# Issuing the last store of a relu-and-sum kernel from ScalarE instead of SyncE

## The chip, the cores and the metric

The kernel runs on one core of a Trainium2 chip. A core has several engines with instruction streams of their own: here VectorE (DVE) and ScalarE (ACT) compute, and SyncE (SP) issues the transfers (DMAs) between the main memory (HBM) and the on-chip memory (SBUF, 128 partitions). The engines are tied together by semaphores: an instruction raises one when it is done, another waits until it has reached a value; a DMA raises its semaphore by 16 when all of it has landed. The metric is the device time of one execution in microseconds (us); less is better.

## The reference

```python
def setup_inputs():
    batch, seq, dim = 32, 512, 1024
    return {"x": np.random.randn(batch, seq, dim).astype(np.float32)}

def reference(x):
    relu_x = np.maximum(x, 0)
    return np.sum(relu_x, axis=-1).astype(np.float32)
```

There are 32 x 512 = 16384 rows of 1024 floats. Each row is clipped at zero and summed to one number. 67 MB go in, 64 KB come out.

## The kernel before

A row is worked on inside one partition, so each of the 128 partitions has J = 128 rows and J results, which are collected in `res` (128 x 128). The rows are divided into three regions of 1, 111 and 16 rows per partition (`REGIONS`), and each region has a store of its own at the end.

The input comes in seven big chunks of 16 rows per partition (8 MB each), into three buffers in turn, and then in a tail of 8, 4 and 2 rows (`TAIL`). The last two rows are cut into four pieces, so that little work is left when the last byte arrives: 912 columns, 512 columns, 256 columns, and a piece of 368 columns that crosses from the one row into the other and goes into a buffer called `seam`. All loads are issued by SP (lines 85 to 115); from the fourth chunk on, SP first waits until DVE has read the buffer that the load is to overwrite.

In the first six chunks ACT clips in place (line 145) and DVE sums (line 160). From the seventh on both engines work on rows of their own: one instruction clips a row and adds it up, followed by a short instruction that reads the accumulator (ACT by `on_act`, line 127; DVE by `on_dve`, line 130).

The end is written out by hand in lines 187 to 209. ACT and DVE each sum half of the 912 columns into `seam` (semaphore `s_half`), ACT the 512 columns and DVE the 256 columns also into `seam` (`s_seam`). Then each engine has one closing instruction, which sums a part of `seam` with those partial sums in it: ACT's gives the result of row J - 2, DVE's that of row J - 1 (lines 201 and 203). Each of the two raises `s_last` by 1.

There are three stores, all issued by SP before the change: the first region in a transposed form (line 117, after `s_turn`), the second region's 111 columns of `res` (line 123, after both engines are done with the last big chunk and the last input piece has landed), and the last region's 16 columns, 8 KB in all (line 207, once `s_last` has reached 2). The first two raise `s_store`, the last one `s_out`. SP ends by waiting for both.

Of the kernel before, what the change touches and what calls it, by code (L numbers as in the profile page):

```python
# [16 lines left out]
def bass_relu_sum_kernel(  # L17
# [20 lines left out]
    J = B * S // P  # L38
# [5 lines left out]
    start = [sum(REGIONS[:i]) for i in range(len(REGIONS))]  # L44
# [4 lines left out]
    ov = [of[P * s : P * (s + n)].rearrange("(p j) -> p j", p=P) for s, n in zip(start, REGIONS)]  # L49
# [4 lines left out]
    res = nc.alloc_sbuf_tensor("res", [P, J], fp32)  # L54
# [10 lines left out]
    s_last = nc.alloc_semaphore("s_last")  # L65
    s_turn = nc.alloc_semaphore("s_turn")
    s_store = nc.alloc_semaphore("s_store")
    s_out = nc.alloc_semaphore("s_out")

    sp, act, dve = nc.sync, nc.scalar, nc.vector  # L70
# [14 lines left out]
    for c in range(NBIG + 1):  # L85
        if c >= NB:
            sp.wait_ge(s_dve, done[c - NB])
        if c < NBIG:
            i = 0
            for g, j, n in CHUNKS[c]:  # L90
                sp.dma_start(  # L91
                    out=buf[:, c % NB, i : i + n, :], in_=xv[g][:, j : j + n, :]
# [18 lines left out]
    for k, (lo, hi) in enumerate((first, second, third)):  # L111
# [6 lines left out]
        out=of[0:P].rearrange("(k q) -> k q", q=32), in_=turned[0:P:32, 0:32]  # L118
# [7 lines left out]
    def on_act(t, acc):  # L126
        return act.activation(t, t, AF.Relu, accum_out=acc)  # L127

    def on_dve(t, acc):
        return dve.tensor_scalar(  # L130
            out=t, in0=t, scalar1=0.0, scalar2=None, op0=ALU.max, op1=ALU.add, accum_out=acc
        )
# [5 lines left out]
    for c in range(NTWO):  # L138
# [17 lines left out]
        for n in DVE_STEPS[c]:  # L156
            if ready[r + n - 1] > seen:
# [3 lines left out]
                out=res[:, c * BIG + r : c * BIG + r + n],  # L161
                in_=buf[:, c % NB, r : r + n, :],
# [36 lines left out]
    act.wait_ge(s_seam, 16 + 2)  # L199
    act.wait_ge(s_half, 2)  # L200
    on_act(seam[:, 0:k], res[:, J - 2 : J - 1]).then_inc(s_last, 1)
    dve.wait_ge(s_seam, 16 + 2)
    on_dve(seam[:, k : k + HEAD + 2], res[:, J - 1 : J]).then_inc(s_last, 1)


    sp.wait_ge(s_last, 2)
    sp.dma_start(out=ov[-1][:, :], in_=res[:, start[-1] : J]).then_inc(s_out, 16)
    sp.wait_ge(s_store, 16 * (len(REGIONS) - 1))
    sp.wait_ge(s_out, 16)

# [27 lines left out]
```

## Time and profile before

| what | us |
|---|---|
| median of three runs | 160.8 (160.7 to 160.84) |
| profiled execution: span, first to last instruction | 159.4 |
| median less that span (start and end of the program) | 1.4 |
| DVE busy | 120.6 |
| ACT busy | 101.5 |
| final store: issue by SP | 0.34 |
| final store: from issue to landing | 1.4 |

The profile is of one execution. Its page gives the span and no time of that execution of its own; the runs give the whole time of other executions of the same program. Times inside the profile count from the first instruction. "SPq" is SP's issue of a DMA, in which the engine gives the transfer out; the transfer itself goes on afterwards, on 16 DMA engines, and the time "to landing" runs from the start of the issue to the last increment of the semaphore. "DMA share" is the mean busy share of those 16 engines. A line such as "DVE res L160" names the engine, the buffer that is written, and the line of the kernel.

### The profile page before, as it was taken

How to read it: one execution, taken by the hardware profiler on the slowest of the kernel's cores; microseconds unless marked ns; L12 is line 12 of the kernel's file. 1: busy time of each engine (PE TensorE's matmuls, PEld its weight loads, DVE VectorE, ACT ScalarE, POOL GpSimd, SP SyncE). 2: the span in 40 equal slices, each digit the busy share in tenths (PEclk: the TensorE clock that was granted, in tenths of full speed). 3: DMA queues.
4: the chain of work that ended last, by engine and by line, in shares of the span. 5: the costliest groups of instructions: out<-in, count | busy, mean ns of one | idle time of the engine just before them, and what ended most of it. 6: DMA issues, size and time to landing. Idle time of an engine off the chain costs nothing.

```text
span 159.4 us, 150 instructions
## 1 busy us (share of the span) xinstructions
DVE 120.6 (76%) x59; ACT 101.5 (64%) x54; POOL 0.2 (0%) x4
## 2 busy tenths in 40 slices
DVE  0000000009999999999999999999999999898995
ACT  3000059980799708996099941999329980496975
POOL 0000000000000000000000000000000000000000
DMA  9997996996996997989979969969969979798994
GB/s 378 493 401 339 493 526 263 526 526 263 526 493 296 526 444 345 526 378 411 526 312 477 526 263 526 526 263 526 526 263 526 444 345 526 321 469 374 417 400 142
DMA packets 2457, 67.18 MB, mean 421 GB/s; under 512 B 536, under 2 KB 792, under 8 KB 1176
## 3 DMA queue, kind: packets, MB, share of 16 engines
q1 hardware_dynamic: 2456, 67.18, 98.1%
q14 instruction: 1, 0.01, 0.0%
HBM read 67.11 MB, written 0.07 MB: 421 GB/s over the span
## 4 chain that ended last, share of the span: by engine, by line
DVE 55%; DMA 34%; ACT 9%; SPq 2%; issue 0%
DVE res L160 54%; DMA buf<-in_x_dram 34%; ACT buf L145 9%; SPq L101 1%; SPq L112 1%; DVE buf L130 0%; DVE seam L130 0%; SPq L91 0%; DVE turned L169 0%
## 5 line engine op out<-in xcount | busy, mean ns | idle before, releaser
L160 DVE TENSOR_REDUCE res<-buf 128x4 f32<-128x4096 f32 (+3 forms) x18 | 99.4, 5596 | 35.5 <-ACT buf L145 35.5
L145 ACT ACTIVATE buf<-buf 128x7168 f32<-128x7168 f32 (+5 forms) x13 | 80.4, 6233 | 46.1 <-DMA buf<-in_x_dram 46.1
L127 ACT ACTIVATE buf<-buf 128x1024 f32<-128x1024 f32 (+2 forms) x19 | 19.0, 999 | 8.9 <-DMA buf<-in_x_dram 8.9
L130 DVE TENSOR_SCALAR_CACHE_REDUCE buf<-buf 128x1024 f32<-128x1024 f32 (+2 forms) x19 | 20.7, 1143 | 1.7 <-DMA buf<-in_x_dram 1.6
L127 ACT ACTIVATION_READ_ACCUMULATOR buf<-buf 128x1 f32 x19 | 3.6, 188 | 0.0
L145 ACT ACT_TABLE_LOAD x1 | 1.3, 1283 | 1.3 <-PEq L223 1.3
L130 DVE DVE_READ_ACCUMULATOR buf<-buf 128x1 f32 x19 | 1.6, 84 | 0.0
L130 DVE TENSOR_SCALAR_CACHE_REDUCE seam<-seam 128x258 f32<-128x258 f32 x1 | 0.4, 421 | 0.0
L127 ACT ACTIVATE seam<-seam 128x114 f32<-128x114 f32 x1 | 0.3, 300 | 0.1
L169 DVE STREAM_TRANSPOSE turned<-res 128x32 f32<-128x32 f32 x1 | 0.2, 211 | 0.0
L127 ACT ACTIVATION_READ_ACCUMULATOR seam<-seam 128x1 f32 x1 | 0.2, 186 | 0.0
L223 POOL MEMSET const-bfloat16-1.0<- 128x1 bf16 x1 | 0.1, 101 | 0.0
L223 POOL MEMSET const-uint8-127<- 128x1 uint8 x1 | 0.1, 101 | 0.0
L223 POOL MEMSET const-float32-0.0<- 128x1 f32 x1 | 0.1, 98 | 0.2 <-issue 0.2
L223 POOL MEMSET const-float32-1.0<- 128x1 f32 x1 | 0.1, 98 | 0.0
L130 DVE DVE_READ_ACCUMULATOR seam<-seam 128x1 f32 x1 | 0.1, 82 | 0.0
## 6 DMA issues: line engine op xcount, KB each, us to landing
buf<-in_x_dram SPq DMA_DIRECT2D x1, 7680.0 KB, 21.1
buf<-in_x_dram SPq DMA_DIRECT2D x1, 4096.0 KB, 25.3
buf<-in_x_dram SPq DMA_DIRECT2D x1, 2048.0 KB, 29.9
buf<-in_x_dram SPq DMA_DIRECT2D x1, 1024.0 KB, 31.9
buf<-in_x_dram SPq DMA_DIRECT2D x1, 512.0 KB, 3.3
buf<-in_x_dram SPq DMA_DIRECT2D x1, 456.0 KB, 32.5
buf<-in_x_dram SPq DMA_DIRECT2D x1, 256.0 KB, 32.7
seam<-in_x_dram SPq DMA_DIRECT2D x1, 184.0 KB, 32.6
```

What stands on the lines that cost most here:

```text
L101: sp.dma_start(out=buf[:, tb, r : r + n, :], in_=xv[-1][:, r : r + n, :]).then_inc(s_in[NBIG + i], 16)
L112: sp.dma_start(out=flat[:, lo:hi], in_=rows[:, lo:hi]).then_inc(s_in[NBIG + len(TAIL) + k], 16)
L127: return act.activation(t, t, AF.Relu, accum_out=acc)
L130: return dve.tensor_scalar(out=t, in0=t, scalar1=0.0, scalar2=None, op0=ALU.max, op1=ALU.add, accum_out=acc)
L145: act.activation(t, t, AF.Relu).then_inc(s_act, 1)
L160: dve.tensor_reduce(out=res[:, c * BIG + r : c * BIG + r + n], in_=buf[:, c % NB, r : r + n, :], axis=X, op=ALU.add,).then_inc(s_dve, 1)
L169: dve.transpose(out=turned[:, :], in_=res[:, 0:32]).then_inc(s_turn, 1)
L223: nc = _bacc.Bacc("TRN2", target_bir_lowering=False, num_devices=1)
```

## The change

The wait for `s_last` and the final store move from SP's instruction stream to ACT's. On ACT they stand behind its closing instruction, which is ACT's last. The store has the same source, destination, size and semaphore; the DMA queue that carries it is now ACT's own, which the kernel has not used until then. SP goes from its store of line 123 to its two closing waits. DVE's and POOL's instructions stay as they are.

```diff
     act.wait_ge(s_seam, 16 + 2)
     act.wait_ge(s_half, 2)
     on_act(seam[:, 0:k], res[:, J - 2 : J - 1]).then_inc(s_last, 1)
+    act.wait_ge(s_last, 2)
+    act.dma_start(out=ov[-1][:, :], in_=res[:, start[-1] : J]).then_inc(s_out, 16)
     dve.wait_ge(s_seam, 16 + 2)
     on_dve(seam[:, k : k + HEAD + 2], res[:, J - 1 : J]).then_inc(s_last, 1)


-    sp.wait_ge(s_last, 2)
-    sp.dma_start(out=ov[-1][:, :], in_=res[:, start[-1] : J]).then_inc(s_out, 16)
     sp.wait_ge(s_store, 16 * (len(REGIONS) - 1))
     sp.wait_ge(s_out, 16)
```

## The prediction

> **What bounds the kernel now.** I read the page's chain first, for what ends last; then the timeline of the last microseconds; then SP's waits; then the load on the DMA engines in short windows around the store. The page's chain says what kind of kernel this is:
>
> ```profile
> span 159.4 us, 150 instructions
> DVE 120.6 (76%) x59; ACT 101.5 (64%) x54; POOL 0.2 (0%) x4
> DVE 55%; DMA 34%; ACT 9%; SPq 2%; issue 0%
> q1 hardware_dynamic: 2456, 67.18, 98.1%
> out_dram<-res SPq DMA_DIRECT2D x1, 8.0 KB, 1.4
> ```
>
> The 16 DMA engines move packets for 98.1% of the span, all in one queue, q1, which SyncE (SP) feeds: the kernel is bound by reading 67 MB. DVE heads the chain only because it gives buffers back to the loads. None of that is touched. The change acts after the last input has been summed, so what counts is the tail, in the timeline (start, duration, engine, line; SPq is SP's issue of a DMA):
>
> ```profile
> 157.01 0.42 DVE L130 TENSOR_SCALAR_CACHE_REDUCE buf<-buf 128x256 f32<-128x256 f32 x1 [0.40 <-DMA buf<-in_x_dram]
> 157.08 0.34 SPq L123 DMA_DIRECT2D out_dram<-res  x1
> 157.19 0.19 ACT L127 ACTIVATION_READ_ACCUMULATOR buf<-buf 128x1 f32 x1
> 157.36 0.08 DVE L130 DVE_READ_ACCUMULATOR buf<-buf 128x1 f32 x1
> 157.47 0.30 ACT L127 ACTIVATE seam<-seam 128x114 f32<-128x114 f32 x1
> 157.47 0.42 DVE L130 TENSOR_SCALAR_CACHE_REDUCE seam<-seam 128x258 f32<-128x258 f32 x1
> 157.68 0.19 ACT L127 ACTIVATION_READ_ACCUMULATOR seam<-seam 128x1 f32 x1
> 157.82 0.08 DVE L130 DVE_READ_ACCUMULATOR seam<-seam 128x1 f32 x1
> 157.93 0.34 SPq L207 DMA_DIRECT2D out_dram<-res  x1
> ```
>
> ACT's closing instruction ends at 157.68 + 0.19 = 157.87, DVE's at 157.82 + 0.08 = 157.90, and SP begins the final store at 157.93. So DVE is the later of the two, and SP loses 0.03 us to the semaphore. SP's waits show what follows:
>
> ```profile
> SPq L122 <- DMA buf<-in_x_dram: 31.0, 1, 31.0
> SPq L209 <- DMA out_dram<-res: 1.1, 1, 1.1
> SPq L207 <- DVE seam L130: 0.5, 1, 0.5
> ```
>
> SP stood waiting for DVE for 0.5 us, so it was ready; after its issue (157.93 + 0.34 = 158.27) it waits 1.1 us for the landing, which brings the end at 159.4. The end is therefore 157.90 + 0.03 + 1.4 (the page's time from issue to landing) + some 0.06 until SP has passed its last wait. Last, the DMA engines over that stretch (window, length, busy time and instructions of DVE, ACT and POOL, clock, DMA share, GB/s):
>
> ```profile
> 157.50:157.90 0.40, 0.40 (x2) 0.36 (x2) 0.00 (x0) 1.00 0.00 0
> 157.90:158.30 0.40, 0.00 (x1) 0.00 (x0) 0.00 (x0) 1.00 0.50 142
> 158.30:158.75 0.45, 0.00 (x0) 0.00 (x0) 0.00 (x0) 1.00 0.00 0
> 158.75:158.85 0.10, 0.00 (x0) 0.00 (x0) 0.00 (x0) 1.00 0.49 45
> 158.85:159.10 0.25, 0.00 (x0) 0.00 (x0) 0.00 (x0) 1.00 0.17 15
> ```
>
> The 55.5 KB store of line 123, issued at 157.08, moves its packets from about 157.90 to 158.30; the final 8 KB store, issued at 157.93, from about 158.8. In between the engines are idle for 0.45 us. Both stores show the same delay from issue to first packet, 0.82 and 0.82 to 0.92 us.
>
> **The change part by part.** The run times are 160.7 to 160.84, median 160.8; the profiled execution has a span of 159.4, so 1.4 us lie around the span (start and end of the program). I add the sum to the span and keep the 1.4 us.
>
> *Removed from SP:* the wait on s_last and one issue of 0.34 us. Both were on the path, as worked out above. SP then goes straight to the waits for s_store and s_out; they end when the final store lands, as before. Nothing else of SP's is behind the removed wait, and no other SP or POOL queue work is passed: the two issues ahead of it in SP's order (lines 117 and 123) are finished at 157.42.
>
> *Added to ACT:* a wait for s_last to reach 2 and one DMA issue. Behind this wait on ACT nothing is queued but the end of the program; ACT would be finished at about 158.3, some 1.1 us ahead of SP, so ACT's own lateness costs nothing unless the issue passes 1.4 us. ACT's closing instruction itself is not delayed, since the wait stands behind it. The wait cannot be satisfied at 157.87 by ACT's own result: it also needs DVE's at 157.90. So the store does not start earlier because ACT "already knows". What is left are three terms.
>
> (a) From DVE's end to the start of the issue: 0.03 us for SP. ACT's own hand-over from DVE is in the same timeline: DVE's read ends at 157.44, ACT's closing instruction starts at 157.47, also 0.03. Ends: -0.03 (none left) and +0.04 (the longest "issue" piece in the chain of waits). I take 0.
>
> (b) The issue itself. No row shows ACT issuing a DMA. SP's rows: 0.327 to 0.343 us when it follows a wait, 0.392 for its very first, 0.43 to 0.46 back to back, 0.633 for line 117. Against the 0.337 of this store the ends are -0.01 and +0.30. I take 0.1, as for the back-to-back rows, between the first-use row and the longest.
>
> (c) From issue to landing in a queue that has carried nothing yet. ACT's queue is used here for the first and only time. The only first use in the trace is SP's first load, 512 KB, issued at 0.00 (windows as above):
>
> ```profile
> 0.00:0.95 0.95, 0.00 (x0) 0.00 (x0) 0.20 (x4) 1.00 0.00 0
> 0.95:1.05 0.10, 0.00 (x0) 0.00 (x0) 0.00 (x0) 1.00 1.55 164
> ```
>
> Its first packet comes about 1.0 us after the issue, against 0.82 to 0.92 for the final store, some 0.13 more (0.06 of it is the longer issue). It lands after 3.3 us; 512 KB at the page's mean of 421 GB/s take 1.25, which leaves 2.05, against 1.4 for the final store: +0.65. That load reads HBM and has another load behind it, so +0.65 is the upper end, and 0 (the new queue behaves like the old) the lower. I take the middle, +0.3, since the row is nearest in being a first use and farther in direction and size.
>
> Sum: 0 + 0.1 + 0.3 = +0.4 us: span 159.8, time 161.2. The ends add up to -0.04 and +0.99, that is 160.8 and 161.8.
>
> [...] Here no issue time is saved, since SP was already waiting. [...]
>
> **The rivals.**
>
> *The same: ACT issues like SP.* Terms (b) and (c) at their lower ends: change of -0.04 to about +0.3, middle 160.9. For it: SP's first issue is only 0.06 us longer than its later ones, and its first packet only 0.13 later; both together give +0.13. Against it: those are rows of SP; ACT issues no DMA anywhere in this trace, and its one issue is at the very end, where nothing covers it.
>
> *Faster: the final store is held in SP's queue by the store ahead of it.* Place: the idle 0.45 us between 158.30 and 158.75. SP's queue still had the 55.5 KB store's completions open there; if the queue held the 8 KB store until then, a queue of its own starts it up to 0.45 us earlier: 160.35. It decides as soon as more than 0.4 of those 0.45 us are such a hold and (b) and (c) are near 0. Against it: the store of line 123 had nothing left ahead of it (the engines are at 0.00 from 157.0 to 157.9) and shows the same 0.82 us, so the idle stretch looks like the plain delay of an issue.
>
> *Slower outside the span.* A second queue might lengthen the start or end of the program, in the 1.4 us that the profile's span does not hold. If it added a fifth to a half of them, +0.3 to +0.7: 161.1 to 161.5, with an unchanged tail. No row speaks for it or against it.
>
> That the change does nothing is not a rival of its own: the wait is where SP's was, so "nothing" is the case of ACT issuing like SP.
>
> **How the numbers follow.** About 0.2% (0.32 us) is what a measurement of this kernel can tell from no change. The forecast (a dearer or cold issue on ACT, above +0.32) gets 0.42; slower outside the span 0.08; together slower 0.50. ACT like SP: 0.35, within 0.2%. Faster by over 0.2%: 0.15, the hold in SP's queue, or a price of ACT's issue below SP's shortest row. The predicted time is that of the likeliest, 161.2; its own range is 161.1 to 161.8. The range that leaves out no more than two in ten goes from 160.4 (nearly the whole hold gone) to 161.9 (upper ends of (a) to (c), with a little outside the span).
>
> **What would show it.** In the profile after, the last DVE line must still end at 157.9 or so. Term (a) is right if ACT's issue starts within 0.05 us of that end. (b) is read from the duration of that issue: near 0.44, against 0.34. (c) is read from its time to landing: 1.8 us with (b) in it, against 1.4; and from the window in which its packets move: about 159.2 instead of 158.8. A second queue must appear beside q1. I am wrong on the slow side if the store lands within 1.4 us; then the time is unchanged. I am wrong the other way if packets of the new queue move at 158.3 to 158.7: then SP's queue held the store. If the span is unchanged and the time is longer, the price lies outside the span.

## The result and the profile after

The changed kernel has a median of 161.04 us (21 runs, 160.81 to 161.86) beside 160.82 for the kernel before (21 runs, 160.70 to 160.92). The ratio is 1.0019, 95% interval 1.0010 to 1.0028: slower by about 0.3 us (the medians differ by 0.22, the means by 0.32), inside the forecast range of 160.4 to 161.9, and just under the 0.2% that counted as a clear change. The 21 runs are of two kinds, so each run's time has to be read beside the span of its profile. For the kernel before, the record has the spans of the 27 runs that went with the first four experiments, and these are of one kind:

| | runs | time less span, us |
|---|---|---|
| kernel before (with the first four experiments) | 27 | 1.31 to 1.41 |
| changed kernel, most runs | 12 | 1.37 to 1.45 |
| changed kernel, late runs | 9 | 1.74 to 2.04 |

The spans of the runs are on record to 0.1 us, so a single value of time less span is good to 0.05 us, and ranges 0.1 us wide can be no more than this rounding. The means are finer (1.36 before, 1.41 for the 12 runs, 1.88 for the 9), and so are the profiled executions, whose spans the trace has to a nanosecond.

The spans of all 21 runs lie at 159.4 to 159.9, mean 159.52, against 159.4 to 159.6, mean 159.48, in the 27 runs before. So some 0.04 us of what the change costs lies in the span, and most of it outside.

Inside the span, the profile after shows the tail as forecast in kind, not in size. The page's span and DMA queues, and the list of DMA issues (size, time from issue to landing):

```profile
span 159.5 us, 150 instructions
q1 hardware_dynamic: 2312, 67.17, 97.9%
q10 hardware_dynamic: 144, 0.01, 0.1%
...
out_dram<-res ACTq DMA_DIRECT2D x1, 8.0 KB, 1.5
```

A second queue, q10, carries the one store. The timeline of the end (start, duration, engine, line; ACTq is ScalarE's issue of a DMA):

```profile
157.15 0.34 SPq L123 DMA_DIRECT2D out_dram<-res  x1
157.25 0.19 ACT L127 ACTIVATION_READ_ACCUMULATOR buf<-buf 128x1 f32 x1
157.42 0.08 DVE L130 DVE_READ_ACCUMULATOR buf<-buf 128x1 f32 x1
157.54 0.30 ACT L127 ACTIVATE seam<-seam 128x114 f32<-128x114 f32 x1
157.54 0.42 DVE L130 TENSOR_SCALAR_CACHE_REDUCE seam<-seam 128x258 f32<-128x258 f32 x1
157.74 0.19 ACT L127 ACTIVATION_READ_ACCUMULATOR seam<-seam 128x1 f32 x1
157.89 0.08 DVE L130 DVE_READ_ACCUMULATOR seam<-seam 128x1 f32 x1
158.00 0.37 ACTq L203 DMA_DIRECT2D out_dram<-res  x1
```

The last input came 0.07 us later in this execution, so all times are to be read from DVE's end (157.89 + 0.08 = 157.97). ACT starts its issue at 158.00, 0.03 us later, as SP did. The issue takes 0.37 instead of 0.34. The trace keeps nanoseconds, where the views print hundredths of a microsecond; in it the store's last increment comes 1.459 us after the start of the issue, against 1.417 before: +0.04, nearly all of it the longer issue. (Its sixteen increments come one by one, over 0.175 us in both profiles.) SP's wait is longer only because it begins earlier:

```profile
SPq L209 <- DMA out_dram<-res: 2.0, 1, 2.0
```

The DMA engines in short windows (window, length, DVE, ACT, POOL busy, clock, DMA share, GB/s) show the store's packets from about 158.9. In the trace the first of them moves 0.88 us after the issue began, against 0.83 from SP, later by what the issue is longer. The idle stretch between the two stores is still there:

```profile
157.90:158.30 0.40, 0.07 (x2) 0.03 (x1) 0.00 (x0) 1.00 0.50 141
158.30:158.75 0.45, 0.00 (x0) 0.00 (x0) 0.00 (x0) 1.00 0.00 1
158.75:158.85 0.10, 0.00 (x0) 0.00 (x0) 0.00 (x0) 1.00 0.00 0
158.85:159.10 0.25, 0.00 (x0) 0.00 (x0) 0.00 (x0) 1.00 0.37 33
```

Behind the store something else has moved. Of the kernel before, the same kind of window at the end:

```profile
159.10:159.40 0.30, 0.00 (x0) 0.00 (x0) 0.00 (x0) 1.00 0.10 27
159.40:160.00 0.60, 0.00 (x0) 0.00 (x0) 0.00 (x0) 1.00 0.00 0
```

and of the changed kernel:

```profile
159.10:159.40 0.30, 0.00 (x0) 0.00 (x0) 0.00 (x0) 1.00 0.00 0
159.40:160.00 0.60, 0.00 (x0) 0.00 (x0) 0.00 (x0) 1.00 0.04 14
```

This is one transfer of 8 KB on a queue whose kind the page of before gives as "instruction"; I call such a transfer a block of instructions:

```profile
q14 instruction: 1, 0.01, 0.0%
```

It starts at 159.21 before, inside the span, and at 159.88 after, outside it (the page after has no q14 line). In both that is 1.23 to 1.24 us after ACT's first increment in the program's end, which is described next (157.98 before, 158.64 after); in the other profiles it is 1.24 to 1.51. That, and the late runs, gave the question for the experiments: is it ACT's late end, the second queue, or something else that lengthens the time outside the span?

One more view is needed. The trace records the increments of a semaphore that no instruction of the kernel raises or waits for. At the end it is raised in two groups of nine; I call them the two rounds of the closing barrier, and the time from one increment to the next a step. What they are for, and which engine makes which increment, the trace does not say. The first of the nine comes at 1.48 us in both profiles; the other eight lie from 157.98 to 159.67 before and from 158.64 to 159.78 after, and the second nine from 160.50 to 160.85 and from 160.61 to 161.01. Two increments of the first round go by their time with an engine. The second comes 0.114 us after ACT's last instruction (157.864 to 157.978 before), and 0.27 us after it where that is the issue of the store (158.374 to 158.644 after): I call it ACT's. The fifth comes 0.12 us after the end of SP's last wait before (159.394 to 159.510) and 0.11 after (159.505 to 159.616): I call it SP's. In the second round, the step to the second increment (ACT's step out) and the step to the eighth (ACT's step back) take 0.034 us each in the kernel before. That these two are ACT's is my reading, from the place of ACT's increment among the nine of the first round. Counted from the first instruction, the measured time ends 0.07 to 0.12 us before the last increment of the second round in twelve of the thirteen profiles with a time of their own.

### The profile page after: what moved, and what is told of

It reads as the page before. It is cut to its first block, busy times and chain, and to the rows that moved or that the text cites. A ratio compares the mean times of both kernels' runs of the same rounds, so it can differ in the third digit from the quotient of the medians.

```text
span 159.5 us, 150 instructions
## 1 busy us (share of the span) xinstructions
DVE 120.6 (76%) x59; ACT 101.5 (64%) x54; POOL 0.2 (0%) x4
## 4 chain that ended last, share of the span: by engine, by line
DVE 55%; DMA 34%; ACT 9%; SPq 2%; issue 0%
DVE res L160 54%; DMA buf<-in_x_dram 34%; ACT buf L145 9%; SPq L101 1%; SPq L112 1%; DVE buf L130 0%; DVE seam L130 0%; SPq L91 0%; DVE turned L169 0%
```

## The experiments

Theory A: the end is longer because ACT reaches it later and its last block of instructions then comes late. Theory B: the second DMA queue lengthens the end. Theory C: only issue and landing count. Theory P came up after the first four runs: the place of ACT's last instructions in its own instruction stream decides.

**ACT held back, no DMA on ACT.** Edit on the kernel before:

```diff
     on_dve(seam[:, k : k + HEAD + 2], res[:, J - 1 : J]).then_inc(s_last, 1)
+    act.wait_ge(s_out, 16)
```

> The kernel before, with one more wait: ScalarE, after its closing instruction, waits for the final store to land (s_out) before it ends. SP issues the store as before; ScalarE has no DMA. Theory A (what counts is when ScalarE reaches the end of its program, because it then fetches a block of 8 KB of instructions that starts about 1.24 us later): the span stays at 159.4, ScalarE ends at about 159.4 instead of 157.9, the fetch starts at about 160.6 to 160.8 instead of 159.2, and the time rises by 0.7 us or more, to 161.5 to 162.5. Theory B (a second DMA queue in the program lengthens its end): there is no second queue here, so 160.8 as before. Theory C (only the dearer issue and landing on ScalarE count): 160.8 as before.

Measured: 161.43 (161.35 to 161.48, 5 runs), before 160.84, ratio 1.0038 (1.0026 to 1.0051); time less span 1.91 to 1.98 in every run; the block of instructions at 160.86. So a late ACT does cost, 0.6 us, a little less than theory A said, and the block comes 0.06 us after its forecast. But the place of the loss was not the one that theory A meant: ACT's step out in the second round took 0.053 us. In the first round the step that follows SP's increment, from the fifth to the sixth, took 0.514 us instead of 0.044, which is 0.47 of the 0.58 us outside the span. The fourth and the sixth increment lie 0.54 us apart there; in the profiled executions of the changed kernel the fifth comes 0.89 us after the fourth (158.73 to 159.62 in the first), and the step behind it takes 0.04. So this loss is not in those executions. None of them is a late one, and no trace shows whether it is in the late ones. Why the step is long with ACT held back, no run shows.

**The second queue in use, ACT not late.** On the kernel before, the first region's small store goes to ACT in mid-stream:

```diff
-    sp.wait_ge(s_turn, 1)
-    sp.dma_start(
-        out=of[0:P].rearrange("(k q) -> k q", q=32), in_=turned[0:P:32, 0:32]
-    ).then_inc(s_store, 16)
...
+        if c == 4:
+            act.wait_ge(s_turn, 1)
+            act.dma_start(
+                out=of[0:P].rearrange("(k q) -> k q", q=32), in_=turned[0:P:32, 0:32]
+            ).then_inc(s_store, 16)
```

> The kernel before, with the small store of the first region (0.5 KB) issued by ScalarE in mid-stream, at about 90 us, instead of by SP; the final store stays with SP. So the second queue is in use and ScalarE has one DMA more, but it reaches the end of its program at 157.9 as before. Theory A: 160.8, the runs within 0.2 us of each other, the fetch of instructions at about 159.2 as before. Theory B: 161.0 or more, with single runs up to 161.9 as in the changed kernel. Theory C: 160.8.

Measured: 161.04 (160.87 to 161.51, 11 runs), ratio 1.0015 (1.0007 to 1.0024); time less span 1.38 to 1.47 in nine runs and 1.90, 1.91 in two. The final store is SP's here and lands after 1.4 us, and ACT leaves the kernel at 157.9:

```profile
q10 hardware_dynamic: 8, 0.00, 0.0%
...
out_dram<-res SPq DMA_DIRECT2D x1, 8.0 KB, 1.4
```

Theories A and C fall: the late runs come without a late ACT. The run fits theory B, and anything else that goes with one more instruction on ACT.

**The queue used before.** The same edit on the changed kernel, so the final store is ACT's second DMA:

> The changed kernel, with the small store of the first region also issued by ScalarE, at about 90 us, so that the final store is the second use of that queue. If a first use costs something (step (c) of the prediction, and part of (b)): the final issue falls from 0.37 to about 0.34 us, issue to landing from 1.5 to 1.4, the span by 0.05 to 0.1. If a first use costs nothing: 0.37 and 1.5 stay. Theory A: in either case single runs up to 161.9 stay, because ScalarE still ends at about 158.4; median 160.9 to 161.1.

Measured: 161.05 (160.85 to 161.25, 11 runs), ratio 1.0014 (1.0005 to 1.0023). The timeline and the list of issues:

```profile
157.97 0.35 ACTq L204 DMA_DIRECT2D out_dram<-res  x1
...
out_dram<-res ACTq DMA_DIRECT2D x1, 8.0 KB, 1.4
```

The issue took 0.353 us, against 0.369 to 0.378 in eight profiles in which it is ACT's first; the last increment came 1.439 after its start, against 1.454 to 1.472 in the eight. So a first use costs about 0.02 us, by this one profile of a used queue, and ACT's issue another 0.01 to 0.02 more than SP's (0.337 to 0.344). The mean span did not change (159.52). Time less span is 1.35 to 1.67 here, mean 1.53, spread rather than in two groups, and no run above 1.7, which I had expected to stay. So there is an excess outside the span here too, 0.17 us in the mean against 0.25 in the first series of the change, and the profiled execution has some of it (1.47), though both of ACT's steps take 0.03 as in the kernel before. Its measured time ends 0.02 us after the last increment, not 0.1 before it, and it is the only trace with a second block of instructions at the end, at 160.77. Whether that block is the reason is not shown.

**Sixteen instructions more on ACT, twice.** On the changed kernel, 32 satisfied waits (the pads), two to an instruction, first in mid-stream, then early (the page of the early one counts 166 instructions, that of the changed kernel 150):

```diff
+        if c == 4:
+            for _ in range(32):
+                act.wait_ge(s_turn, 1)
```

> The changed kernel, with 32 waits more on ScalarE that are already satisfied (s_turn reached 1 at 70 us), at about 90 us, where ScalarE idles. Theory A with the fetch triggered at the end of the program: nothing changes, 161.0, with runs up to 161.9. Theory A with the fetch triggered by a place in ScalarE's instruction stream (every so many instructions): the fetch moves ahead of the tail, the runs above 161.2 vanish and the median is 160.85 to 160.95. Theory B: 161.0, with runs up to 161.9.

```diff
             on_act(*row(c, i))
+        if c == 0:
+            for _ in range(32):
+                act.wait_ge(s_in[0], 16)
```

> The changed kernel with 32 satisfied waits (16 instructions, each with two) more on ScalarE, now right after its first big instruction, ahead of its wait for the second chunk. Theory P (place: what lengthens the end of single runs is where ScalarE's last instructions fall in its instruction stream, since the end of the program then needs a block that is still being fetched): time less span 1.3 to 1.4 in every run, as with the later padding. The later padding added 0.3 us to the span; if that was delay of ScalarE's work in mid-stream, it is smaller here, span 159.5 to 159.6, and the time 160.85 to 161.0. Theory B (a second queue lengthens the end): single runs with 1.7 to 2.0 between span and time.

Measured: 161.16 (161.02 to 161.23, 11 runs) and 161.11 (161.01 to 161.28, 11 runs); ratios 1.0021 (1.0012 to 1.0029) and 1.0016 (1.0006 to 1.0025). Time less span is 1.31 to 1.40 in all 22 runs: no run is late, and the small excess is gone, with the second queue in use and ACT as late as in the change. For the small excess theory B falls. For the late runs the 0 of 22 decides less, since the changed kernel itself showed none when it ran again (below). The spans are longer instead, 159.7 to 159.9 against 159.5, which no theory had forecast, so both medians lie above what was expected. They are as long with the early pads as with the later ones, so it is not ACT's delay in mid-stream. The page of the early one:

```profile
span 159.7 us, 166 instructions
q14 instruction: 1, 0.01, 0.0%
```

This block of instructions moves at 141.8, in the midst of the loads; another one follows at 160.07, outside the span, 1.26 us after ACT's first step in the end of the program, much as in the changed kernel. The last load in the chain of waits, of the changed kernel, of the early pads and of the pads in mid-stream:

```profile
124.42 32.63 DMA buf<-in_x_dram
```

```profile
124.39 32.83 DMA buf<-in_x_dram
```

```profile
124.28 33.08 DMA buf<-in_x_dram
```

The extra 0.20 and 0.45 us here, 0.3 in the mean of the spans, is near what a packet of 8 KB takes on one DMA engine: 0.31 us is the median of the 128 such packets of the loads in the profile after, and the block at its end took 0.42 (0.49 before). That an engine's load waits for it is my estimate from these numbers; no run separates it.

**One instruction more on ACT, no second queue.** On the kernel before:

```diff
             on_act(*row(c, i))
+        if c == 0:
+            for _ in range(2):
+                act.wait_ge(s_in[0], 16)
```

> The kernel before, SP with all stores, no second queue, with one instruction more on ScalarE, early: a wait that is already satisfied. ScalarE's stream is then as long as in the changed kernel. Theory P: single runs with 1.7 us or more between span and time, as in the changed kernel (9 of 21) and with the early store on ScalarE (2 of 11); median 160.85 to 161.1. Theory B: 1.3 to 1.4 in every run, median 160.84, as in the kernel before.

Measured: 160.99 (160.84 to 161.09, 11 runs), before 160.88, ratio 1.0006 (0.9998 to 1.0015). Time less span 1.38 to 1.46, mean 1.41 against 1.37 before; ACT's step out in the second round took 0.081 instead of 0.034 us, as in the changed kernel (0.081 to 0.090 in five profiles). So the small excess, 0.04 us in the usual runs, needs neither the queue nor the store: one instruction more on ACT brings it. The late runs (1.7 and more), which theory P expected, did not come.

**One instruction fewer on ACT, store on ACT's queue.** On the changed kernel:

```diff
-    on_act(flat[:, lo : CUT // 2], seam[:, 0:1]).then_inc(s_half, 1)
-    on_dve(flat[:, CUT // 2 : hi], seam[:, 1:2]).then_inc(s_half, 1)
+    on_act(flat[:, lo : CUT // 2], seam[:, 0:1]).then_inc(s_seam, 1)
+    on_dve(flat[:, CUT // 2 : hi], seam[:, 1:2]).then_inc(s_seam, 1)
...
-    act.wait_ge(s_seam, 16 + 2)
-    act.wait_ge(s_half, 2)
+    act.wait_ge(s_seam, 16 + 4)
...
-    dve.wait_ge(s_seam, 16 + 2)
+    dve.wait_ge(s_seam, 16 + 4)
```

> The changed kernel with one waiting instruction fewer on ScalarE: the two half sums count on s_seam instead of s_half, so the closing instruction waits for one semaphore (s_seam at 20) instead of two. ScalarE's stream is then as long as in the kernel before, with the store still on its queue. Theory P (place in ScalarE's stream, together with the store): the excess over the kernel before that stays in every run falls by about 0.05 us, ScalarE's step in the closing barrier goes back from 0.083-0.090 to 0.034 us, and no run has 1.7 us or more between span and time; median 160.85 to 160.95. Theory B (the second queue alone): 3 to 5 of 11 runs with 1.7 us or more, median 160.95 to 161.2.

Measured: 160.88 (160.78 to 161.08, 11 runs), before 160.89, ratio 0.9999 (0.9990 to 1.0008). Time less span 1.31 to 1.41, mean 1.37, as before; ACT's step out is back at 0.034 us. (The 0.04 us that the store itself takes longer are less than this interval, some 0.14 us to each side, can tell.) The timeline shows the store still issued by ACT, at the same price:

```profile
157.82 0.08 DVE L130 DVE_READ_ACCUMULATOR seam<-seam 128x1 f32 x1
157.94 0.38 ACTq L202 DMA_DIRECT2D out_dram<-res  x1
```

**The same edit on the kernel before**, as its control (the same lines, the store with SP):

> The kernel before, SP with all stores, with the two half sums counted on s_seam, so with one waiting instruction fewer on ScalarE. It tells whether that edit gains anything by itself, and so how the changed kernel with the same edit is to be read (it ran level with the kernel before). If the edit only undoes the late block of instructions in the changed kernel: nothing to undo here, 160.8 to 160.9, ratio 0.9990 to 1.0005. If it shortens the tail by itself: the closing instructions start earlier after the last partial sum, or ScalarE's end is earlier, and the time falls by 0.05 us or more.

Measured: 161.00 (160.96 to 161.19, 11 runs), before 160.87, ratio 1.0008 (0.9999 to 1.0017). This is more than the expected 160.8 to 160.9. Time less span is 1.46 to 1.55 in all 11 runs, against 1.31 to 1.41: the end is 0.13 us longer in the mean without any DMA on ACT. In the second round ACT's step out takes 0.034, its step back 0.156 us. The tail inside the span is not shorter: SP's issue starts 0.03 us after DVE's end as ever. So the edit gains nothing by itself, and that the changed kernel is level with it fits the length of ACT's stream, which is then as it was before.

**The changed kernel again**, three single executions, to have the profile of a late one, and one series of 11 runs on the chip of the run with one fewer:

> The changed kernel as it is, for the profile of another execution. In about 4 of 10 executions the time lies 1.7 to 2.0 us above the span instead of 1.4. If this is one of them: Theory P expects ScalarE's last block of instructions to be fetched late and the gap in the semaphores of the closing barrier to be at ScalarE's step. Theory B expects it elsewhere. If it is not one of them: 160.8 to 161.0, as in the profile that is there.

> The changed kernel as it is, once more, for the same purpose and with the same expectations: either 160.8 to 161.0 with 1.4 us between span and time, or 161.2 to 161.9 with 1.7 to 2.0.

> The changed kernel as it is, on the same chip as the one with an instruction fewer, so that the share of its late executions is known there: 3 to 5 of 11 with 1.7 us or more between span and time, median 160.9 to 161.1, if the share is that of its first runs (9 of 21); fewer if it depends on the chip.

> The changed kernel as it is, for the profile of one more execution: 160.8 to 161.0 with 1.4 us between span and time, or, in about 4 of 10 executions, 161.2 to 161.9 with 1.7 to 2.0. In the late case the closing barrier is expected to wait for ScalarE some 0.5 us.

Measured: 160.93, 160.91 and 160.94; the series 160.96 (160.88 to 161.19, 11 runs), before 160.89, ratio 1.0003 (0.9994 to 1.0012). None of these 14 runs is late (time less span 1.37 to 1.46; 1.40 to 1.41 in the profiled executions, against 1.37 with one instruction fewer), where 9 of the first 21 were. So there is no profile of a late execution. Taken together (ACT instructions against the kernel before; ACT's steps in the second round, in us, from one profile of each):

| kernel | ACT instr. | DMA on ACT | time less span, usual | runs of 1.7 or more | step out | step back |
|---|---|---|---|---|---|---|
| before | 0 | no | 1.31 to 1.41 | 0 | 0.034 | 0.034 |
| changed | +1 | yes | 1.37 to 1.45 | 9 of 21 | 0.083 | 0.034 |
| changed, again (series) | +1 | yes | 1.37 to 1.46 | 0 of 11 | 0.081 | 0.034 |
| before, ACT held back | +1 | no | 1.91 to 1.98 | 5 of 5 | 0.053 | 0.035 |
| early store on ACT | +1 | yes | 1.38 to 1.47 | 2 of 11 | 0.106 | 0.035 |
| before, one more | +1 | no | 1.38 to 1.46 | 0 of 11 | 0.081 | 0.034 |
| changed, one fewer | 0 | yes | 1.31 to 1.41 | 0 of 11 | 0.034 | 0.034 |
| before, one fewer | -1 | no | 1.46 to 1.55 | 0 of 11 | 0.034 | 0.156 |
| both stores on ACT | +2 | yes | 1.35 to 1.67 | 0 of 11 | 0.035 | 0.034 |
| changed, pads in mid-stream | +17 | yes | 1.32 to 1.40 | 0 of 11 | 0.035 | 0.034 |
| changed, early pads | +17 | yes | 1.31 to 1.40 | 0 of 11 | 0.034 | 0.034 |

## Why the prediction was right, and where it was wrong

The time lies in the range and the direction is right, but the likeliest case was not what happened. The rival "slower outside the span", to which I gave 0.08, carried most of the cost, so it is luck that the sum of 161.2 came near the 161.04.

- *What bounds the tail* held: DVE's end, a hand-over of 0.03 us, the store, SP's wait. Term (a) is 0 as taken (its upper end should have been 0.05, the longest "issue" piece, not 0.04).
- *Term (b)*, ACT's issue, was taken as +0.1 and measured +0.035 (0.372 against 0.337). The row that fitted was SP's own after a wait, not the back-to-back rows, of which the prediction gave 0.43 to 0.46; two more, among the first four loads, took 0.42 and 0.50.
- *Term (c)*, the first use of a queue, is where the sum failed: taken as +0.3 from SP's first load, it measured under 0.01 us between this store and SP's beyond the longer issue, and a used queue gained 0.02. What made the load's 3.3 us was not looked into; it reads, and has another load behind it. (b) and (c) together are +0.04, not +0.4; that is the rival "ACT issues like SP" inside the span.
- *The faster rival* falls: the packets came 0.88 us after the issue from a queue with nothing ahead in it too, against 0.83 from SP's, so the idle 0.45 us was no hold by the store ahead.
- *"ACT's own lateness costs nothing"* held in the kernel's code; I did not look beyond it. The prediction called q1 the only queue, although the page of before has the line of q14. ACT's one instruction more moves its last instructions in its stream, and with it ACT's step in the closing barrier takes about 0.05 us longer and the usual runs about 0.04. The runs with one more, one fewer and sixteen more show that the number of ACT's instructions, and neither queue nor store, sets this part. Why it does stays open. That the step waits for the block of instructions is not shown, and its times speak against it: the block had landed 0.31 us before the slow step out began in the changed kernel, and 0.19 us before the normal one with one fewer; in the kernel before with one fewer it had landed about 1 us before the slow step back.
- *The late runs* make up the rest. With 9 of 21 some 0.5 us longer, they add about 0.2 us to the mean; with 0.04 inside the span and 0.05 outside in the mean of the others that is the 0.3 us of the ratio. What they are stays open. Apart from the kernel that holds ACT back, they came only in kernels that issue a DMA on ACT and have exactly one ACT instruction more (9 of 21 and 2 of 11), though with both stores on ACT eight of 11 runs lie between, at 1.51 to 1.67. The changed kernel showed none in 14 later runs; the series of 11 among them had the ratio 1.0003. A thing that differs between series must take part in them. It may be the chip: that of the first series is not on record, the early store's two late runs came on one on which two single executions of the changed kernel were not late, and the series of 11 ran on another. Without late runs the change costs some 0.1 us, less than such a series can tell.

What a block of instructions costs, the runs do not settle. In mid-stream the spans with an extra block (8 KB on q14) were 0.3 us longer, which fits a cost; at the end of the program a shift by one instruction goes with 0.04 to 0.13 us, but no trace shows that a block is the reason.

## What to carry to other kernels

Before a store is moved to another engine's queue, look whether the old engine is late in issuing it; here SP stood ready for 0.5 us, so there was nothing to gain, and ACT's issue cost 0.02 to 0.04 us more. When an effect is a few tenths of a microsecond, compare each run's time with its span before explaining anything: here most of the difference lay outside the span. And try a null edit of the same length (one satisfied wait more, or one fewer) before a change of that size is put down to what it does.

## What the runs showed of the hardware that was not expected

- The time outside the span changed with the number of instructions of ACT: time less span has the mean 1.37 us at the old count, 1.40 to 1.43 with one more (usual runs), 1.49 with one fewer and 1.35 with sixteen more in addition to the store. With two more, both stores on ACT, it is 1.53 and spread, and ACT's steps in the barrier do not show why.
- Eight kilobytes on the instruction queue during the loads (at 141.8 with the early pads) went with 0.3 us more span (159.8 in the mean of 11 runs each, against 159.5).
- Holding ACT at the end of the kernel until the final store had landed cost 0.6 us although SP waited for the same store: one step in the barrier, the one behind SP's increment, took 0.51 us instead of 0.04. Why is not shown: the increments on the two sides of SP's lay 0.54 us apart there, and 0.93 in the changed kernel, where that step took 0.04.
